# S5 input tables used inside the table loop: ten of sixteen go from on-chip memory straight into V's products

## The chip, the cores and the metric

One NeuronCore of a Trainium2 chip runs the whole program. The metric is the device time in microseconds of one execution; lower is better.

## What is computed

One layer of a hybrid encoder on 2048 tokens of width 1024, in float32: a normalisation, one input projection, two mixers side by side, an output projection, and a gated feed-forward network. Only the start of the S5 mixer matters here:

```
bur = einsum('blgc,gpc->lbgp', u, bbr)        # 32 groups g of 16 channels c, 64 states p
bui = einsum('blgc,gpc->lbgp', u, bbi)
h   = associative_scan(h[t] = a * h[t-1] + bu[t])     # complex; forward and backward
y   = Re(C h) + D u
```

The kernel cuts time into 128 blocks of 16 steps. For each pair of groups it makes a table of powers of `a` times `B`; the product of that table with the `u` values of a block is the block's input `V` to a short recursion over the 128 blocks.

## The kernel before

The program is written for a tile framework: each line names an engine, the framework places semaphores, and a list scheduler fixes the order of each engine's instructions by priority. `soon()` gives a block the priority of an early point of the program (`p0`), so that its instructions go ahead of what stands before them in the text as soon as they are ready. Each engine, and SP with the DMAs that it issues, then works through its own list in order.

A memory pool has an address range. Pools are stacked on a left and on a right side; a pool that is opened on addresses of a closed one waits for everything that used the closed one. That matters for five pools. `s0` (left) holds the weights and buffers of the projection `u_dt`. `s5cs` and `s5tab` (right) hold the constants and the working tiles of the tables. `s5v` (left) holds `V`, and `dts` and `s5vw` (left, above it) the working tiles of `dt_stage` and of `inputs`; these three take the place of `s0`. `sp` (right), which holds the working tiles of the SSD units, reaches the addresses of `dts` and `s5vw`.

The order of the work around the change:

- `norm_block` and `u_dt`, four blocks of 512 tokens: normalise, transpose on PE, project. `u` goes to DRAM (`u_d`).
- `tables(k)` for k = 0 to 15, two groups each. DVE makes `X` (three operations for each of real and imaginary part, L254 to L256). PE transposes it (L264), ACT copies the transposed table out of PSUM into `xin` (L265; one buffer), and SP stores it to DRAM (`s5xd`, 512 KB, L266). Further parts of the same call make a 64-column product for the convolution kernel `kt` (`s5cp`, L272; `s5pk`, L277 to L285) and the output table `s5O` (POOL and DVE, L238 to L243), which is stored in four pieces (L294). `kt` lives in the two buffers of `rb`, which the convolution of the SSD part needs later.
- `z_tile` for m = 0 to 3: large products that depend on none of this and fill PE's gaps.
- `dt_stage` (DVE, a chain of small operations; ACT; four small stores): the time steps of the SSD part, `tokS` and `acs_d`.
- `toeplitz`: 30 small stores of `kt` from POOL's queue (L308, L310).
- `inputs`: for eight blocks b, load `uT` from `u_d` (L318) and twice a stored table `s5xi` from `s5xd` (L322; three buffers); 16 products of 128x128x128 on PE (L329) into `s5pv`; ACT copies one half of the rows into `V` (L333), DVE the other half, reversed in time (L334).
- `recur`: 126 steps of four POOL operations on `V` (L347 to L350), paced along the SSD groups of the second half of the sequence.
- `group(1, g)`: four convolution tiles (products `pmm` into `rb`, L679, and DVE) and eight SSD units; the units load rows of `acs_d` into `rw` (L747) and begin on PE with `ptb` (L756). z tiles 4 to 7 fill in. After that come the first half of the sequence, the output projection and the feed-forward network.

Of the kernel before, what the change touches and what calls it, by code (L numbers as in the profile page):

```python
# [17 lines left out]
P = 128  # L18
# [11 lines left out]
GA = 4  # L30
ZB = ((4,), (5,), (6,), (7,))
# [71 lines left out]
class S5:  # L103
# [141 lines left out]
    def tables(self, wk, k):  # L245
# [20 lines left out]
        nc.sync.dma_start(self.xd[k], xin.rearrange("p q d m -> p (q d m)"))  # L266
# [46 lines left out]
    def inputs(self, vp, wk):  # L313
        nc = self.nc
        self.V = vp.tile([P, 2, NG5, P], F32, name="s5V")
        for b in range(8):
            uT = wk.tile([P, 8, P], F32, name="s5uT", bufs=2)
            nc.sync.dma_start(uT, self.ud[4 * b:4 * b + 4].rearrange("g h p c -> p (g h) c"))  # L318
            for kk in range(2):
                k = 2 * b + kk  # L320
                xin = wk.tile([P, 1024], F32, name="s5xi", bufs=3)
                nc.sync.dma_start(xin, self.xd[k])  # L322
                xin = xin.rearrange("p (r h g m) -> p r h g m", r=2, h=2, g=2)
                pv = self.pst("s5pv")
                for r in range(2):
                    for g in range(2):
                        o = 128 * (2 * r + g)
                        for h in range(2):
                            nc.tensor.matmul(pv[:, o:o + 128], xin[:, r, h, g],  # L329
                                             uT[:, 2 * (2 * kk + g) + h], start=(h == 0), stop=(h == 1))  # L330
                V = self.V[:, :, 2 * k:2 * k + 2, :]
                pvv = pv.rearrange("p (r g c) -> p r g c", r=2, g=2)
                nc.scalar.copy(V[0:64], pvv[0:64])  # L333
                nc.vector.tensor_copy(V[64:128, :, :, ::-1], pvv[64:128])  # L334

# [862 lines left out]
def hybrid_block_kernel(ctx: ExitStack, tc: tile.TileContext, *aps):  # L1198
# [9 lines left out]
    with ExitStack() as mix:  # L1208
# [18 lines left out]
        with pool(name="s0", bufs=1) as sp, right("s5cs") as cs:  # L1227
# [19 lines left out]
            with right("s5tab") as wk:  # L1247
                with soon():
                    for k in range(NK5):
                        s5.tables(wk, k)  # L1250
                for m in range(ZA):
                    b.z_tile(wp, ps, ht, 1, m)
        late = rs.enter_context(right("late"))
        mp = rs.enter_context(right("mp"))
        with pool(name="s5v", bufs=1) as vp, ExitStack() as xs:
            off = tc.cur_priority - p0
            with tc.high_priority(offset=off), pool(name="dts", bufs=1) as sp:
                b.dt_stage(late, sp, ps)
                with pool(name="s5vw", bufs=1) as wk:
                    s5.toeplitz(*[wk.tile([P, 1024], F32, name="s5xi", bufs=3)[0:16, 0:512].rearrange(  # L1260
                        "p (g o) -> p g o", o=16) for _ in range(2)])
                    s5.inputs(vp, wk)
            sp = rs.enter_context(right("sp"))
            xp = xs.enter_context(pool(name="s5xa", bufs=1))
            b.masks(late)
            b.sb = late.tile([P, 4, 256], F32, name="sb")
            p0 = tc.cur_priority
            for g in range(GA):
                if g == GA - 1:
                    p3 = tc.cur_priority  # L1270
                b.group(mp, wp, sp, ps, pp, ht, 1, g)
                for m in ZB[g]:
                    b.z_tile(wp, ps, ht, 1, m)
# [3 lines left out]
            with tc.high_priority(offset=tc.cur_priority - p3):  # L1277
                for j in range(2):
                    b.norm_again(xp, wp, ps, ht, j, 2 + 512 * j)
# [91 lines left out]
```

## Time and profile before

| what | value |
|---|---|
| time, median of 3 runs | 2923.3 us (2913.18 to 2929.7) |
| profiled execution: its own time | 2930.28 us |
| profiled execution: span | 2928.5 us |
| PE busy | 2701.5 us, 92% of the span |
| DVE busy | 2197.4 us, 75% |
| ACT busy | 1364.4 us, 47% |
| POOL busy | 653.9 us, 22% |
| TensorE clock granted, mean | 0.968 |

A busy PE is an upper bound: the ends of matmuls are modelled and overlap, so starts say more than durations. The spans of POOL are rough.

### The profile page before, as it was taken

Reading aid. Unit: us, or ns where it says so; the run is one execution under the profiler, and the core shown is the slowest. Engines: PE = TensorE matmul, PEld = TensorE weight load, DVE = VectorE, ACT = ScalarE, POOL = GpSimd, SP = SyncE. Lnnn points to the kernel's source line nnn. Section 1 sums busy time; section 2 is a strip of 40 time slices with the busy share of each in tenths; the row PEclk is TensorE's granted clock in tenths of the full one; section 3 lists DMA queues with packets and bytes.
Section 4 is the critical chain, followed back from the end, with each engine's and each line's share of the span. In section 5 each row is a group of like instructions: output and inputs, shape, how many; then the busy total and the mean of one; then the engine's idle time right before and its main releaser. Section 6 shows DMA issues by size and latency. Waiting matters only on the chain.

```text
span 2928.5 us, 37294 instructions
## 1 busy us (share of the span) xinstructions
PE 2701.5 (92%) x12952; PEld 2181.7 (74%) x12952; DVE 2197.4 (75%) x3255; ACT 1364.4 (47%) x2329; POOL 653.9 (22%) x1133
## 2 busy tenths in 40 slices
PE   6998899876999998899898999999999999999997
PEld 4666899765877886677776878787877777877776
DVE  5997688786786776677767777779887888656587
ACT  4542455444567665334235444446444445333254
POOL 0443499992233332111120000000000000000012
PEclk9999999988999999999998999999999999999999
DMA  4546633448455656957845234325444337456464
GB/s 129 173 133 198 168 114 121 112 128 227 134 175 162 188 163 204 252 170 201 252 141 187 79 108 137 107 77 193 149 136 130 121 131 243 160 204 194 150 233 158
DMA packets 507400, 471.55 MB, mean 161 GB/s; under 512 B 90364, under 2 KB 417356, under 8 KB 507212
## 3 DMA queue, kind: packets, MB, share of 16 engines
q1 hardware_dynamic: 504972, 463.99, 52.4%
q0 software_dynamic: 2240, 5.18, 0.7%
q8 instruction: 102, 1.67, 0.2%
q14 instruction: 86, 0.70, 0.1%
HBM read 324.37 MB, written 144.67 MB: 160 GB/s over the span
## 4 chain that ended last, share of the span: by engine, by line
PE 40%; DMA 8%; DVE 7%; issue 2%; ACT 2%; POOL 1%; SPq 0%; ACTq 0%; DVEq 0%; POOLq 0%
PE pA L1040 17%; PE pB L1040 9%; PE pD L1040 5%; PE p L444 3%; PE p L445 2%; PE p L446 2%; DMA ar<-act_d 2%; DVE ll L440 1%; DMA bs<-in_ffn_w_down_dram 1%; DMA wr<-in_ffn_w_up_dram 1%; DMA bs<-hop_d 1%; DMA wt_d<-bs 1%; PE po L846 1%; DVE tl L1027 1%; DMA tst<-in_ffn_w_down_dram 0%
## 5 line engine op out<-in xcount | busy, mean ns | idle before, releaser
L1040 PE MATMUL pA<-th,lh 128*128 128x512 f32 x1056 | 423.7, 402 | 28.3 <-ACT pc L1088 18.8
L1040 PE MATMUL pA<-tl,lh 128*128 128x512 f32 x1056 | 422.1, 400 | 4.2 <-DVE tl L1027 4.2
L1040 PE MATMUL pA<-th,ll 128*128 128x512 f32 x1056 | 420.5, 399 | 0.8 <-DVE ll L440 0.8
L444 PE MATMUL pmm<-hh,wh 128*128 128x512 f32 (+1 forms) x896 | 333.9, 373 | 3.7 <-DVE zt L706 2.4
L445 PE MATMUL pmm<-hl,wh 128*128 128x512 f32 (+1 forms) x896 | 332.7, 371 | 0.0
L446 PE MATMUL pmm<-hh,wl 128*128 128x512 f32 (+1 forms) x896 | 330.2, 369 | 0.0
L1040 PEld LDWEIGHTS pA<-th,lh 128*128 128x128 f32 x1056 | 200.6, 190 | 86.7 <-ACT pc L1088 27.4
L1040 PEld LDWEIGHTS pA<-tl,lh 128*128 128x128 f32 x1056 | 200.7, 190 | 54.2 <-DVE tl L1027 6.4
L1040 PEld LDWEIGHTS pA<-th,ll 128*128 128x128 f32 x1056 | 200.6, 190 | 50.3 <-DVE ll L440 1.6
L1040 PE MATMUL pB<-tl,lh 128*128 128x512 f32 x528 | 209.6, 397 | 1.8 <-DVE tl L1027 1.8
L1040 PE MATMUL pB<-th,lh 128*128 128x512 f32 x528 | 209.7, 397 | 1.8 <-ACT lh L439 1.6
L1040 PE MATMUL pB<-th,ll 128*128 128x512 f32 x528 | 209.2, 397 | 0.0
L1088 ACT COPY pc<-pA 128x512 f32<-128x512 f32 x204 | 116.0, 584 | 185.4 <-PE pA L1040 184.4
L444 PEld LDWEIGHTS pmm<-hh,wh 128*128 128x128 f32 x896 | 169.9, 190 | 30.2 <-issue 3.7
L445 PEld LDWEIGHTS pmm<-hl,wh 128*128 128x128 f32 x896 | 169.8, 190 | 22.6 <-issue 2.5
L764 ACT ACTIVATE Lt<-rw,tokS 128x128 f32<-128x128 f32 x512 | 157.4, 389 | 61.3 <-PE pyd L770 48.7
L446 PEld LDWEIGHTS pmm<-hh,wl 128*128 128x128 f32 x896 | 169.6, 189 | 21.3 <-issue 1.1
L692 DVE SCALAR_TENSOR_TENSOR xbc<-rb,cw,xbc 128x1024 f32<-128x1024 f32 x128 | 178.7, 1399 | 3.8 <-ACT xbc L690 2.8
L444 PE MATMUL p<-wo,yh 128*128 128x512 f32 x384 | 157.3, 410 | 22.2 <-ACT yh L439 21.3
L439 ACT CAST lh<-s 128x512 fp32r<-128x512 f32 (+3 forms) x136 | 109.1, 815 | 123.8 <-DVE s L1007 71.2
L440 DVE TENSOR_TENSOR ll<-s,lh 128x1024 fp32r<-128x1024 f32 (+3 forms) x136 | 126.3, 933 | 52.5 <-PE pA L1040 43.7
L445 PE MATMUL p<-wo,yh 128*128 128x512 f32 x384 | 155.6, 405 | 0.0
(421 smaller groups left out, 6139.0 us busy)
## 6 DMA issues: line engine op xcount, KB each, us to landing
wr<-in_ffn_w_up_dram SPq DMA_DIRECT2D x88, 512.0 KB
rw<-acs_d SPq DMA_DIRECT2D x128, 256.0 KB
wraw<-in_w_in_dram SPq DMA_DIRECT2D x52, 512.0 KB
ar<-act_d SPq DMA_DIRECT2D x32, 512.0 KB
yp_d<-cv SPq DMA_DIRECT2D x32, 512.0 KB
cv<-yp_d SPq DMA_DIRECT2D x32, 512.0 KB
tst<-hop_d SPq DMA_DIRECT2D x28, 512.0 KB
act_d<-cv SPq DMA_DIRECT2D x22, 512.5 KB
```

What stands on the lines that cost most here:

```text
L439: self.nc.scalar.copy(hi, src)
L440: self.nc.vector.tensor_tensor(lo, src, hi.bitcast(F32), ALU.subtract)
L444: mm(ps, lhs[0], rhs[0], start=first, stop=False)
L445: mm(ps, lhs[0], rhs[1], start=False, stop=False)
L446: mm(ps, lhs[1], rhs[0], start=False, stop=last)
L692: nc.vector.scalar_tensor_tensor(ac, rb[:, j:j + 1024], cw(j), ac, ALU.mult, ALU.add)
L764: nc.scalar.activation(Lt[:, d, h], rw[:, d, h], AF.Exp, bias=tk(0, d, h))
L846: nc.tensor.matmul(po[:, 2 * (g - 2 * q) + j], self.fst[:, g, 128 * j:128 * j + 128], ct[:, g], start=True, stop=True)
L1027: nc.vector.tensor_tensor(l, st[:, 0:n], h.bitcast(F32), ALU.subtract)
L1040: mm(ps, x, y, start=first and k == i == 0, stop=k == kt - 1 and i == 2, skip_group_check=not first)
L1088: self.nc.scalar.copy(t, src)
```

## The change

- `tables(k)` takes an optional `uT`. With it, the transposed table is not stored to DRAM; `input(k, xin, uT)` multiplies it with `u` at once and copies the result into `V`.
- The first KD = 6 tables go to DRAM as before, in pool `s5tab`. Then `V` is allocated, and tables 6 to 15 run in a second pool `s5tab2` on the same addresses, with `uT` loaded per pair of tables (b = 3 to 7). After tables 7, 9 and 11 the stored tables 0 to 5 are loaded again in pairs and used (`stored`; two buffers).
- The products go into a PSUM buffer of the pool `pp` (tag `tb`, two buffers) instead of `s5ps`.
- Both copies into `V` are on ACT; before, the reversed half was on DVE.
- z tiles 0 and 1 stay in the first block, 2 and 3 move into the second.
- `dt_stage` and `toeplitz` come behind all of this, and their pools `dts` and `s5tp` now take the addresses of the closed `s5vw`. `toeplitz` gets two tiles of its own. `s5cs` closes after the second block.

```diff
-        nc.sync.dma_start(self.xd[k], xin.rearrange("p q d m -> p (q d m)"))
+        if uT is None:
+            nc.sync.dma_start(self.xd[k], xin.rearrange("p q d m -> p (q d m)"))
+        else:
+            self.input(k, xin, uT)
...
+    def load_u(self, wk, b):
+        uT = wk.tile([P, 8, P], F32, name="s5uT", bufs=2)
+        self.nc.sync.dma_start(uT, self.ud[4 * b:4 * b + 4].rearrange("g h p c -> p (g h) c"))
+        return uT
+
+    def input(self, k, xin, uT):
+        nc = self.nc
+        pv = self.pp.tile([P, 512], F32, name="s5pv", tag="tb", bufs=2)
+        for r in range(2):
+            for g in range(2):
+                o = 128 * (2 * r + g)
+                for h in range(2):
+                    nc.tensor.matmul(pv[:, o:o + 128], xin[:, 4 * r + 2 * h + g].rearrange("p d m -> p (d m)"),
+                                     uT[:, 2 * (2 * (k % 2) + g) + h], start=(h == 0), stop=(h == 1))
+        V = self.V[:, :, 2 * k:2 * k + 2, :]
+        pvv = pv.rearrange("p (r g c) -> p r g c", r=2, g=2)
+        nc.scalar.copy(V[0:64], pvv[0:64])
+        nc.scalar.copy(V[64:128, :, :, ::-1], pvv[64:128])
+
+    def stored(self, wk, k):
+        xin = wk.tile([P, 8, 2, 64], F32, name="s5xi", bufs=2)
+        self.nc.sync.dma_start(xin.rearrange("p q d m -> p (q d m)"), self.xd[k])
+        return xin
...
             with right("s5tab") as wk:
                 with soon():
-                    for k in range(NK5):
+                    for k in range(KD):
                         s5.tables(wk, k)
-                for m in range(ZA):
+                for m in range(ZA // 2):
                     b.z_tile(wp, ps, ht, 1, m)
+        vp = vpo.enter_context(pool(name="s5v", bufs=1))
+        s5.V = vp.tile([P, 2, NG5, P], F32, name="s5V")
+        with right("s5tab2") as wk, pool(name="s5vw", bufs=1) as vw:
+            with soon():
+                for k in range(KD, NK5):
+                    if k % 2 == 0:
+                        uT = s5.load_u(vw, k // 2)
+                    s5.tables(wk, k, uT)
+                    j = (k - KD) // 2
+                    if k % 2 and j < KD // 2:
+                        uT = s5.load_u(vw, j)
+                        for kk in (2 * j, 2 * j + 1):
+                            s5.input(kk, s5.stored(vw, kk), uT)
+            for m in range(ZA // 2, ZA):
+                b.z_tile(wp, ps, ht, 1, m)
+        cso.close()
...
-                with pool(name="s5vw", bufs=1) as wk:
-                    s5.toeplitz(*[wk.tile([P, 1024], F32, name="s5xi", bufs=3)[0:16, 0:512].rearrange(
-                        "p (g o) -> p g o", o=16) for _ in range(2)])
-                    s5.inputs(vp, wk)
+            with pool(name="s5tp", bufs=1) as wk:
+                s5.toeplitz(*[wk.tile([P, 512], F32, name="s5z", bufs=2)[0:16].rearrange(
+                    "p (g o) -> p g o", o=16) for _ in range(2)])
```

## Rows read from the trace of the kernel before

**Rows 1.** Windows: us; busy (count) of PE, PEld, DVE, ACT, POOL; clock, DMA, GB/s.

```profile
80.00:209.00 129.00, 119.10 (x592) 77.82 (x591) 118.37 (x142) 66.86 (x163) 63.32 (x64) 0.97 0.55 159
209.00:262.00 53.00, 50.34 (x222) 36.19 (x221) 51.40 (x86) 14.97 (x38) 14.97 (x16) 0.97 0.52 151
262.00:330.00 68.00, 51.77 (x348) 48.77 (x348) 27.52 (x46) 19.26 (x32) 20.41 (x36) 0.90 0.81 237
660.00:700.00 40.00, 19.03 (x107) 14.60 (x107) 23.64 (x48) 19.82 (x50) 12.84 (x20) 0.71 0.90 251
```

**Rows 2.** Groups of instructions by line, 262 to 330 us.

```profile
L329 PE MATMUL s5pv<-s5uT,s5xi 128*128 128x128 f32 x256 | 34.7, 300 | 13.9 <-DMA s5xi<-s5xd 13.9
L334 DVE COPY s5V<-s5pv 64x512 f32<-64x512 f32 x16 | 11.0, 694 | 29.2 <-ACT s5V L333 29.1
L333 ACT COPY s5V<-s5pv 64x512 f32<-64x512 f32 x16 | 9.2, 575 | 32.8 <-PE s5pv L329 32.8
```

**Rows 3.** Timeline of PE around `inputs`: start, us, instruction, idle before it.

```profile
268.80 3.73 PE L329 MATMUL s5pv<-s5uT,s5xi 128*128 128x128 f32 x32
...
320.22 0.31 PE L444 MATMUL pmm<-hh,wh 128*128 128x342 f32 x1
...
320.68 0.32 PE L444 MATMUL pmm<-hh,wh 128*128 128x342 f32 x1
...
325.41 2.02 PE L329 MATMUL s5pv<-s5uT,s5xi 128*128 128x128 f32 x16 [0.48 <-DMA s5xi<-s5xd]
```

**Rows 4.** Groups of PE by line and shape, 268.8 to 329.3 us.

```profile
L444 PE MATMUL pmm<-hh,wh 128*128 128x342 f32 x16 | 5.4, 340 | 0.0
```

**Rows 5.** Timeline of SP's queue: stores and loads.

```profile
185.65 0.55 SPq L266 DMA_DIRECT2D s5xd<-s5xin  x1
...
210.07 1.35 SPq L565 DMA_DIRECT2D u_d<-us  x2
...
217.00 1.05 SPq L318 DMA_DIRECT2D s5uT<-u_d  x2
...
256.68 0.32 SPq L266 DMA_DIRECT2D s5xd<-s5xin  x1
...
327.46 0.80 SPq L747 DMA_DIRECT2D rw<-acs_d  x2
```

**Rows 6.** Groups of ACT by line, 80 to 262 us.

```profile
L265 ACT COPY s5xin<-s5pxt 128x512 f32<-128x512 f32 x32 | 17.2, 590 | 13.9 <-PE s5pxt L264 13.9
L272 ACT ACTIVATE s5cp<-s5ct 64x32 f32<-64x32 f32 x64 | 14.6, 228 | 5.9 <-POOL s5cp L268 5.0
L280 ACT COPY s5ks<-s5pk 64x256 f32<-64x256 f32 x16 | 5.9, 367 | 2.9 <-PE s5pk L277 1.8
L285 ACT COPY rb<-s5pk 128x64 f32<-128x64 f32 x30 | 4.9, 219 | 13.6 <-PE s5pk L283 13.5
L705 ACT ACTIVATE zt<-pmm 128x512 f32<-128x512 f32 x6 | 3.6, 596 | 18.9 <-DMA z_d<-zt 16.4 <-PE pmm L446 2.5
```

**Rows 7.** Timeline of POOL: first and last of `toeplitz`, start of `recur`.

```profile
262.83 1.49 POOL L308 DMA_DIRECT2D s5td<-rb  x2 [6.89 <-ACT rb L285]
...
284.81 0.62 POOL L310 DMA_DIRECT2D s5td<-rb  x1 [0.60 <-DMA s5td<-rb]
...
329.32 0.35 POOL L347 TENSOR_TENSOR s5r<-s5V,s5ar 128x64 f32<-128x64 f32 x1 [24.74 <-DVE s5V L334]
```

**Rows 8.** Timeline of DVE: first and last of 68 operations of `dt_stage`.

```profile
216.36 0.33 DVE L595 TENSOR_REDUCE dtm<-ident 128x1 f32<-128x64 f32 x2
...
303.16 1.23 DVE L616 TENSOR_TENSOR_SCAN dtq<-dtz,dte 128x512 f32<-128x512 f32 x1
...
314.12 0.69 DVE L633 TENSOR_TENSOR dtq<-dtq,dte 128x512 f32<-128x512 f32 x1
```

**Rows 9.** Instructions of one line: duration min/median/max in ns, first and last start.

```profile
L254 DVE TENSOR_TENSOR s5tmw<-s5pw,s5bb x32: 678/691/1759, 80.4 to 248.4; 128x512 f32<-128x512 f32 x32
```

**Rows 10.** Instructions of tile `ptb`, 300 to 450 us, same columns.

```profile
L756 PE MATMUL ptb<-ident,xbc x24: 270/272/273, 372.9 to 428.8; 128*128 128x128 f32 x24
```

More of the change, by code (lines that the diff above doesn't have):

```diff
@@ L30 @@
 GA = 4
+KD = 6
 ZB = ((4,), (5,), (6,), (7,))
@@ L243, in outer, with tables @@
             eng.tensor_tensor(out, out, tm, op)
-    def tables(self, wk, k):
+    def tables(self, wk, k, uT=None):
         nc, ident = self.nc, self.ident
@@ L311, in toeplitz @@
                               self.kt[1][112 - 16 * (l % 8):128 - 16 * (l % 8), 1 - l // 8])
-    def inputs(self, vp, wk):
-        nc = self.nc
[L315 to L334, printed above, removed]
@@ L1226, in hybrid_block_kernel @@
             "p (h g o) -> p h g o", h=2, o=16) for _ in range(2)]
-        with pool(name="s0", bufs=1) as sp, right("s5cs") as cs:
+        cso, vpo, xs = ExitStack(), ExitStack(), ExitStack()
+        cs = cso.enter_context(right("s5cs"))
+        with pool(name="s0", bufs=1) as sp:
             with right("s5prm") as sr:
@@ L1253, in hybrid_block_kernel @@
+        cso.close()
         late = rs.enter_context(right("late"))
         mp = rs.enter_context(right("mp"))
[L1255 to L1258, printed above, removed]
-                with pool(name="s5vw", bufs=1) as wk:
-                    s5.toeplitz(*[wk.tile([P, 1024], F32, name="s5xi", bufs=3)[0:16, 0:512].rearrange(
-                        "p (g o) -> p g o", o=16) for _ in range(2)])
-                    s5.inputs(vp, wk)
[L1263 to L1273, printed above, removed]
-            p1 = tc.cur_priority
-            s5.recur(vp, lambda j: tc.high_priority(offset=tc.cur_priority - p0 - int(RS * (p1 - p0) * j / P)))
-            s5.store_states()
-            with tc.high_priority(offset=tc.cur_priority - p3):
-                for j in range(2):
-                    b.norm_again(xp, wp, ps, ht, j, 2 + 512 * j)
@@ new lines, in hybrid_block_kernel @@
+        off = tc.cur_priority - p0
+        with tc.high_priority(offset=off), pool(name="dts", bufs=1) as sp:
+            b.dt_stage(late, sp, ps)
+            with pool(name="s5tp", bufs=1) as wk:
+                s5.toeplitz(*[wk.tile([P, 512], F32, name="s5z", bufs=2)[0:16].rearrange(
+                    "p (g o) -> p g o", o=16) for _ in range(2)])
+        sp = rs.enter_context(right("sp"))
+        xp = xs.enter_context(pool(name="s5xa", bufs=1))
+        b.masks(late)
+        b.sb = late.tile([P, 4, 256], F32, name="sb")
@@ new lines, in hybrid_block_kernel @@
+        p0 = tc.cur_priority
+        for g in range(GA):
+            if g == GA - 1:
+                p3 = tc.cur_priority
+            b.group(mp, wp, sp, ps, pp, ht, 1, g)
+            for m in ZB[g]:
+                b.z_tile(wp, ps, ht, 1, m)
+        p1 = tc.cur_priority
+        s5.recur(vp, lambda j: tc.high_priority(offset=tc.cur_priority - p0 - int(RS * (p1 - p0) * j / P)))
+        s5.store_states()
+        with tc.high_priority(offset=tc.cur_priority - p3):
+            for j in range(2):
+                b.norm_again(xp, wp, ps, ht, j, 2 + 512 * j)
@@ L1280, in hybrid_block_kernel @@
+        xs.close()
+        vpo.close()
         with right("s5o") as so:
```

## Prediction

> **What bounds the kernel now.** I read the busy time by window first, for the stage in which the change lies. From 80 to 262 us two engines are full: DVE is busy for 118.4 of 129 and 51.4 of 53 us, PE for 119.1 and 50.3 [rows 1]. That is the stage of `u_dt` and the tables. From 262 to 330 us nothing is full but the DMA: PE 51.8 of 68 us at a clock of 0.90, DVE 27.5, DMA share 0.81 [rows 1]. That is `inputs`. From 330 us on PE is nearly full again. So what can be won lies between 262 and 330 us.
>
> The groups of that window say what PE waits for: 13.9 us before the products of `inputs`, for the load of `s5xi` [rows 2]. DVE and ACT wait there for the products in turn (29.2 and 32.8 us). The timeline of PE gives the work itself. All 256 products lie between 268.8 and 327.4 us; 32 of them in a row take 3.73 us, 16 take 2.02 [rows 3], so 16 sets take 16 x 1.95 = 31 us. Into the same stretch the scheduler mixed 48 matmuls of the first convolution tile, 16 of each of three kinds [rows 4]; one of each kind starts every 0.46 us [rows 3], so these are 16 x 0.46 = 7.4 us. The eight transposes of `dt_stage` are about 8 x 0.12 = 1 us, an estimate from the products, which have the same shape. Of 268.8 to 329.3 us, 60.5 us, that leaves 60.5 - 31 - 7.4 - 1 = 21 us in which PE did nothing, or worked at a lower clock.
>
> DVE shows a second effect of the same loads. `dt_stage` is a chain on DVE. It begins at 216.4 us, beside the tables, but its scan starts only at 303.2, since the copies into `V`, which wait for products that wait for loads, stand ahead of it in DVE's list; it ends at 314.8 [rows 8]. The SSD units' first load of `rw` is issued at 327.46 us, just as the last product ends [rows 3, 5]: its pool takes the place of `s5vw`.
>
> **The change part by part.** *Removed:* ten stores and ten loads of 512 KB, six stores and loads stay. Ten of the 16 loads that PE waited for are gone, and the other six and all eight loads of `uT` move to a stage with a DMA share of 0.52 [rows 1]. This takes away the wait for loads. It doesn't shrink PE's work: the 31 us of products go into a stage in which PE has only 129 - 119.1 + 53 - 50.3 = 12.6 us free. They push the z tiles, PE's filler, back by as much. So the gain is the 21 us that PE lost, and up to 21 + 12.6 = 34 us if the products also fill every gap before.
>
> *Moved: when can it begin?* `V` and `uT` take the place of `s0`, so no product can run before `u_dt` has ended and its last store has landed. Before, the last store of u is issued at 210.07 us and the first load of `uT` at 217.00 [rows 5]. Table 9 was stored at 185.65 us [rows 5], so the old loop was at about table 12 then. The new loop has one buffer `xin`: table 6 fills it, tables 7 to 9 can be made up to their transposes and `X` buffers, then DVE has no more `X` to make until about 214 us (217 less the few us by which `u_dt` ends earlier when DVE and PE are free for it). What hides this is the rest of the tables: the output parts (`s5O`) need no `xin` and can be made meanwhile. PE has `u_dt` and z tiles. I cost it at nothing on PE; without that cover PE would stand from u's last store to the first `uT`, 7 us [rows 5]. The change of pool after table 5 stops DVE for a few us; PE again has `u_dt`.
>
> *Added: the chain per table on ACT.* ACT gets the reversed copy too. Per table: `xin` 2 x 0.590, two copies into `V` 2 x 0.575 (the row of the unreversed copy [rows 2]; a reversed one on DVE took 0.694), `s5cp` 4 x 0.228, `s5ks` 0.367, `rb` 2 x 0.219 [rows 6], together 1.18 + 1.15 + 0.91 + 0.37 + 0.44 = 4.05 us. From 214 us: nine tables, 36.5 us, six stored tables, 6 x 1.15 = 6.9, and eight activations of z tiles, 8 x 0.596 = 4.8 [rows 6]; 48.2 us, and with the casts of the z weights some 52. So the last table's `V` is ready at 214 + 52 = 266 us if ACT never waits. Before, the last table was stored at 256.7 us [rows 5] and `V` was complete at 329.3 [rows 7]. Bounds for the nine tables: DVE alone, six `X` of six operations of 0.691 [rows 9], 25 us, gives 240 at the earliest; the old pace, (256.7 - 185.65) / 6 = 11.8 us a table [rows 5], would give 214 + 9 x 11.8 = 320 at the latest. I take 266, nearer to the lower end, since the old pace was that of a DVE that also had `dt_stage`, norms and whole tables to do, and here the rest waits on ACT alone.
>
> *What is late next.* `rb` comes free when `toeplitz` is stored: 30 POOL issues from 262.83 to 285.43 us [rows 7], 22.6 us, and the landing, for which I take 5.6 us, the time from the end of the last store of u to the first load of `uT` [rows 5]: 266 + 28 = 294 us. Until then PE has z tiles: they end where the products begin, at 268.8 us [rows 3], and with 31 us of products ahead of them at 300. So `rb` doesn't hold the convolution, PE does; it starts at about 300, where before, with its 7.4 us of early work put in one piece, it started at 329.3 - 7.4 = 321.9. `dt_stage` now begins when `s5vw` is free, at 266 us: 68 operations whose durations add up to 37.6 us [rows 8], and 3.5 us of waits (the 13 from the scan on, 8.2 us, took 11.6), 307 us. From its end to the first load of `rw` it was 327.5 - 314.8 = 12.7 us [rows 5, 8], so `rw` loads at 320. The first SSD product on PE came at 372.9 us [rows 10], so at 352 with 21 us gained; that leaves 32 us. `recur` starts at about 295 instead of 329.3 us.
>
> Here a rule speaks against the change. Where POOL works beside it, an operation of a table on DVE takes up to 1759 ns instead of 678 [rows 9], and `recur` on POOL may now run beside the end of `dt_stage`. The Trainium skill (SBUF — State Buffer, "Who interferes with whom") says that DVE instructions with two inputs in SBUF and GpSimd instructions that read SBUF take turns, each blocked while the other runs. By that row at its worst, `dt_stage` would take 37.6 x 1759 / 678 = 98 us and end at 364, and the first SSD product would be no earlier than before; by its median of 691 ns it ends at 307 and is hidden. I take it near the lower end, since most of it is over before `recur` can begin at 295.
>
> **Sum.** 2930.3 us (the profiled execution) - 21 = 2909. The profiled execution lies 7 us over the median of the runs, so the median should be 2923.3 - 21 = 2902 us. About 0.5%, 14.6 us, is what a measurement of this kernel can tell from no change.
>
> **Rivals.**
> - *More is gained, 2880.* The products fill the 12.6 us of gaps too, and `recur` ends earlier within the SSD groups. Between 660 and 700 us, when the states are stored at a DMA share of 0.90, PE is busy for 19 of 40 us at a clock of 0.71 [rows 1]; with other work at hand half of that, 10 us, goes. 21 + 12.6 + 10 = 43 us. Against it: a schedule seldom fills all gaps, and the stores collide with something else.
> - *Late tables or a slow `dt_stage`, 2913.* If the chain takes 7.9 us a table, `V` is ready at 214 + 9 x 7.9 = 285, `rb` free at 313, and 322 - 313 = 9 us, about 10, are left; a `dt_stage` stretched by `recur` gives the same. For it: single buffers (`xin`, `s5cp`) and ACT's list in order. Time: 2913, no change that can be told.
> - *Slower, 2938: the one buffer `xin` becomes the bound.* Each table waits for the products of the one before, and these stand in PE's list behind z matmuls. The change loses when a table takes over (322 - 28 - 214) / 9 = 8.9 us; at 10.5 us, below the old 11.8, `V` comes at 308.5, `rb` at 336.5, and the convolution 15 us late. For it: the old pace. Against it: no DVE work like that is left.
>
> **How the numbers follow.** Chances: the forecast 0.45 (its own range 2890 to 2912), more gained 0.15, late tables 0.26, slower 0.14. Faster by over 0.5% (under 2908.7): 0.15 and 0.41 of the forecast's 0.45, 0.56. Same: 0.04 + 0.26 = 0.30. Slower: 0.14. The range reaches from the larger gain, 2878, to a loss of 9 us, 2932, which leaves out the upper half of the slower cases and what lies beyond the larger gain.
>
> **What would show it.** Right: between 262 and 330 us no wait of PE for `s5xi`, ten stores and loads fewer, last copies into `V` at 260 to 275 us, first convolution matmuls near 300, DVE's `dt_stage` unbroken after the last table, and everything behind shifted by some 20 us. Wrong: `V` ready after 285, PE idle between 185 and 300, a convolution that waits for `rb`, a `dt_stage` that ends after 330, or a shift that is gained at 300 and given back by 700, with the stores of the states at another place.

## The result and the profile after

The change makes the kernel slower. The kernel after takes 2956.4 us (median of four runs, 2953.6 to 2958.9), the kernel before 2925.4 in the runs beside it; 31 us by the medians, and the ratio is 1.0113, interval 1.008 to 1.0145. The spans of the profiled executions, 2951.5 and 2928.5 us, differ by 23 us. The two medians come from four runs each; in the four later sets of runs the kernel before took 2934 to 2937 us, and the kernel after was not timed there, so that the 31 us are the less certain of the two figures. Lines of the kernel after lie about five below those of before (L444 is L449, L649 is L654).

The windows of the kernel after, columns as in [rows 1], with two more of 20 us:

```profile
209.00:262.00 53.00, 52.80 (x365) 45.10 (x363) 35.11 (x43) 27.84 (x62) 13.96 (x12) 1.00 0.63 192
262.00:330.00 68.00, 26.29 (x165) 21.50 (x163) 48.65 (x90) 19.64 (x42) 34.37 (x60) 0.74 0.39 76
300.00:320.00 20.00, 0.00 (x0) 0.00 (x0) 19.45 (x39) 0.00 (x0) 8.86 (x16) 0.50 0.26 23
320.00:340.00 20.00, 8.64 (x44) 8.45 (x45) 10.03 (x17) 5.83 (x8) 16.70 (x41) 0.61 0.26 51
660.00:700.00 40.00, 19.99 (x92) 14.39 (x88) 23.25 (x39) 17.61 (x39) 0.00 (x0) 0.53 0.66 189
```

From 262 to 330 us the DMA share has fallen from 0.81 to 0.39, as it should with ten stores and ten loads gone. But PE is busy for 26.3 us where it was for 51.8 [rows 1], and from 300 to 320 us it does nothing at all, while DVE is full. The timeline of PE says what it stands for:

```profile
288.51 1.95 PE L329 MATMUL s5pv<-s5uT,s5xin 128*128 128x128 f32 x16
...
331.36 1.09 PE L654 MATMUL ptd<-ident,dtq 128*128 128x128 f32 x4 [40.90 <-DVE dtq L638]
332.24 1.06 PE L654 MATMUL ptd<-ident,dtw 128*128 128x128 f32 x4
333.12 0.65 PE L449 MATMUL pmm<-hh,wh 128*128 128x342 f32 x1
```

The last product ends at 290.5 us. The next instructions in PE's list are the eight transposes of `dt_stage`, and they wait 40.9 us for the last operation of its chain on DVE. In the kernel before the same wait is 2.3 us:

```profile
314.86 1.11 PE L649 MATMUL ptd<-ident,dtq 128*128 128x128 f32 x4 [2.32 <-DVE dtq L633]
```

The convolution stands behind the transposes in the list. It begins at 333.1 us, where the prediction had 300 and the kernel before an equivalent 321.9. The chain itself, on DVE, SP, ACT and POOL (four fences: SP's queue, DVE's first and last operation of the chain, ACT, POOL):

```profile
290.49 0.35 SPq L591 DMA_DIRECT2D dtpr<-in_ssd_dt_bias_fwd_dram  x1
...
336.87 0.81 SPq L752 DMA_DIRECT2D rw<-acs_d  x2
```

```profile
291.30 0.34 DVE L600 TENSOR_REDUCE dtm<-ident 128x1 f32<-128x64 f32 x2
...
330.40 0.81 DVE L638 TENSOR_TENSOR dtq<-dtq,dte 128x512 f32<-128x512 f32 x1
```

```profile
291.09 0.58 ACT L334 COPY s5V<-s5pv 64x512 f32<-64x512 f32 x1
325.67 0.20 ACT L644 ACTIVATE dtde<-dtend 128x4 f32<-128x4 f32 x1 [34.00 <-DVE dtend L630]
```

```profile
286.91 1.49 POOL L312 DMA_DIRECT2D s5td<-rb  x2 [8.99 <-ACT rb L289]
...
306.94 0.67 POOL L314 DMA_DIRECT2D s5td<-rb  x1
307.58 0.43 POOL L352 TENSOR_TENSOR s5r<-s5V,s5ar 128x64 f32<-128x64 f32 x1
307.98 0.78 POOL L353 TENSOR_TENSOR s5r<-s5V,s5ai 128x64 f32<-128x64 f32 x1
318.81 0.52 POOL L619 MEMSET dtz<- 128x512 f32 x1 [10.05 <-issue]
...
642.33 0.74 POOL L361 DMA_DIRECT2D s5vd<-s5V  x1 [0.29 <-POOL s5V L355]
```

The pool `dts` lies on the addresses of `s5vw`, so the first load of `dt_stage` goes out when the last product has ended; the chain takes 331.2 - 291.3 = 39.9 us and has almost nothing beside it on DVE (three operations of `toeplitz`, 0.67 us each). ACT waits 34 us of it. POOL stands 10 us of it too: `recur` begins at 307.6 us instead of 329.3 [rows 7], but a memset of `dt_stage` stands in POOL's list ahead of its third operation. `recur` stores its states 20 us earlier, from 642.3 us instead of 662.1, and no time comes of it. The first SSD product on PE comes at 389.4 us; before it was 372.9 [rows 10]:

```profile
L761 PE MATMUL ptb<-ident,xbc x24: 270/272/328, 389.4 to 446.4; 128*128 128x128 f32 x24
```

### The profile page after: what moved, and what is told of

Same layout as the page of the kernel before. It is cut to its first block, busy times and chain, and to the rows that moved or that the text cites. A ratio compares the mean times of both kernels' runs of the same rounds, so it can differ in the third digit from the quotient of the medians.

```text
span 2951.5 us, 37284 instructions
## 1 busy us (share of the span) xinstructions
PE 2692.1 (91%) x12952; PEld 2176.3 (74%) x12952; DVE 2190.5 (74%) x3239; ACT 1374.5 (47%) x2345; POOL 644.5 (22%) x1133
## 4 chain that ended last, share of the span: by engine, by line
PE 65%; DVE 13%; DMA 12%; ACT 4%; issue 3%; POOL 2%; SPq 1%; ACTq 0%; DVEq 0%; POOLq 0%
PE pA L1045 18%; PE pB L1045 9%; PE pD L1045 5%; PE pmm L449 5%; PE pmm L450 5%; PE pmm L451 5%; PE p L449 2%; PE p L450 2%; PE p L451 2%; DMA ar<-act_d 2%; DMA rw<-acs_d 1%; PE s5py L391 1%; DVE ll L445 1%; DMA s5uTo<-u_d 1%; PE pst L796 1%
## 5 line engine op out<-in xcount | busy, mean ns | idle before, releaser
L449 PE MATMUL pmm<-hh,wh 128*128 128x512 f32 (+1 forms) x896 | 333.9, 373 | 7.6 <-ACT rb L684 4.5
L449 PEld LDWEIGHTS pmm<-hh,wh 128*128 128x128 f32 x896 | 170.3, 190 | 33.5 <-ACT rb L684 5.8
L449 PE MATMUL p<-wo,yh 128*128 128x512 f32 x384 | 157.5, 410 | 21.9 <-ACT yh L444 21.9
L444 ACT CAST lh<-s 128x512 fp32r<-128x512 f32 (+3 forms) x136 | 109.1, 815 | 129.0 <-DVE s L1012 67.6
```

The lines of the kernel that those rows point to most:

```text
L444: self.nc.scalar.copy(hi, src)
L449: mm(ps, lhs[0], rhs[0], start=first, stop=False)
```

## The experiments

Theory A: what costs is `dt_stage`, whose chain now begins only behind the last product and whose transposes stand ahead of the convolution in PE's list. Rival B: the pace of the tables (8.8 us each, with one buffer `xin`) and behind it `rb`. Sixteen kernels were timed, each in runs beside the kernel before, to which the ratio is taken (its median is 2934 to 2937 us there, and 2925 us beside the kernel after). All results in one table, with what the traces show: the end of the last copy into `V`, the first SSD transpose on PE (`ptb`), and PE's busy time from 200 to 400 us.

| kernel | ratio (interval) | last V | first `ptb` | PE 200:400 |
|---|---|---|---|---|
| before | 1 | 329.2 | 372.9 | 179.9 |
| after | 1.0113 (1.008 to 1.0145) | 291.7 | 389.4 | 152.2 |
| e1 own addresses for `dts` | 1.0015 (0.9999 to 1.003) | 310.4 | 381.7 | 166.0 |
| e2 before, `dt_stage` behind | 1.0152 (1.0127 to 1.0176) | 309.2 | 415.8 | 135.5 |
| e3 `ptd` behind two tiles | 1.0010 (0.9994 to 1.0025) | 293.5 | 376.0 | 168.7 |
| e4 two `xin` | 1.0050 (1.0033 to 1.0068) | 286.1 | 386.4 | 160.9 |
| e5 six z tiles | 1.0089 (1.0054 to 1.0124) | 293.8 | 400.3 | 164.9 |
| e6 before, six z tiles | 1.0045 (1.0025 to 1.0066) | 342.4 | 385.9 | 182.6 |
| e7 e1, six z tiles | 1.0071 (1.0043 to 1.0098) | 313.0 | 391.2 | 178.0 |
| e8 e7, two `xin`, stores split | 1.0060 (1.0039 to 1.008) | 303.3 | 390.9 | 177.9 |
| e9 e8, four z tiles | 1.0023 (1.0003 to 1.0042) | 306.8 | 377.5 | 173.6 |
| e10 e3, z weights late, `dt_stage` later | 0.9992 (0.9976 to 1.0008) | 278.1 | 375.1 | 172.4 |
| e11 e3, two `xin`, stores split | 1.0021 (1.0007 to 1.0035) | 284.3 | 379.8 | 165.7 |
| e12 e10 and e11 | 0.9991 (0.997 to 1.0011) | 273.9 | 380.2 | 169.2 |
| e13 z tiles last | 1.0042 (1.0022 to 1.0061) | 276.3 | 381.6 | 165.2 |
| e14 e3 and e13 | 0.9969 (0.9949 to 0.9989) | 278.9 | 365.8 | 180.7 |
| e15 e14, two `xin`, stores split | 0.9999 (0.9979 to 1.0019) | 272.3 | 367.5 | 177.1 |
| e16 e1, e13, two `xin`, stores split | 1.0027 (1.0014 to 1.004) | 304.6 | 381.3 | 175.1 |

In fifteen of these seventeen kernels the time follows the first `ptb`: its shift against the kernel before and the difference of the two medians agree within 6 us (e2: 43 and 43 us; e14: -7 and -8.5 us). So what a kernel loses or gains is settled, for the most part, before the first SSD product. The exceptions are e12 (+7 us of shift, -4 us of time) and the kernel after (16.5 us of shift, 31 us of time); measured from the 2934 to 2937 us of the later sets, the kernel after would be 20 to 22 us slower and fit.

**The first four: which of the two it is.** e1 opens the pool `dts` between `s5v` and `s5vw`, so that it shares no address with the latter:

```diff
         s5.V = vp.tile([P, 2, NG5, P], F32, name="s5V")
+        dto = ExitStack()
+        dsp = dto.enter_context(pool(name="dts", bufs=1))
         with right("s5tab2") as wk, pool(name="s5vw", bufs=1) as vw:
...
-        with tc.high_priority(offset=off), pool(name="dts", bufs=1) as sp:
-            b.dt_stage(late, sp, ps)
+        with tc.high_priority(offset=off):
+            b.dt_stage(late, dsp, ps)
```

> The changed kernel with one thing undone: the pool of the dt stage has addresses of its own beside those of s5vw, so that its chain on DVE can run between the tables as it did before the change. Theory A (the order of the dt stage costs the time: its chain begins only when s5vw is free at 291 us, and its transposes stand in PE's list ahead of the first convolution): the 40.9 us in which PE stands before the transposes of ptd shrink to what the release of rb asks, the last copy into V at 291 to 300 us, the first convolution matmul at 312 to 321 us instead of 333, and the time falls from 2956 to 2931 to 2948. Rival B (the pace of the tables, 8.8 us each with one buffer xin, is the bound): the 38 us of the dt stage on DVE push the tables back by as much, the last copy into V at 320 us or later, and the time stays at 2950 to 2965.

e2 does the reverse to the kernel before: `dt_stage` behind `inputs`, on the addresses of their closed pool.

```diff
-            with tc.high_priority(offset=off), pool(name="dts", bufs=1) as sp:
-                b.dt_stage(late, sp, ps)
+            with tc.high_priority(offset=off):
                 with pool(name="s5vw", bufs=1) as wk:
                     s5.toeplitz(...)
                     s5.inputs(vp, wk)
+                with pool(name="dts", bufs=1) as sp:
+                    b.dt_stage(late, sp, ps)
```

> The kernel before with one part of the change alone: the dt stage is moved behind the inputs, on the addresses that their pool s5vw has left; tables, stores and loads stay as they were. Theory A: the chain on DVE begins at about 329 us, where the last product ends, PE stands for some 40 us before the transposes of ptd, the convolution starts at about 370 us instead of 329, and the time rises from 2925 to 2955 to 2970, more than the whole loss of the change. Rival B: the chain is hidden in front of the first SSD unit, and the time stays within 0.5% of 2925.

e3 leaves the chain where it is and moves only its last step, the transposes, behind the second convolution tile (the tiles `dtq` and `dtw` get a pool of their own that stays open until then):

```diff
-        for kd, src in enumerate((ln, w)):
+        self.lnw = (ln, w)
+    def dt_turn(self, ps):
+        for kd, src in enumerate(self.lnw):
             pt = ps.tile([P, 512], F32, name="ptd", tag="mm")
...
         for i, (mt, c0) in enumerate(cols):
             sl.append(self.conv_tile(mp, wp, ps, ht, half, mt, c0))
+            if mid and i == 1:
+                mid()
```

> The changed kernel with only the list of PE altered: the eight transposes of ptd, with their two copies, stand behind the first two convolution tiles, and the chain of the dt stage itself keeps its addresses and its start at 291 us. Theory A in the form that PE's list is what costs: the convolution starts when rb is free, at about 310 to 314 us instead of 333, PE stands for 20 us instead of 41, and the time falls by 15 to 21 us to 2935 to 2941. Theory A in the form that the chain itself is too late for the SSD units: the first SSD transposes stay at 389 us and the time within 0.3% of 2956. Rival B (rb or the tables hold the convolution): the first convolution matmul stays at 330 us or later, and the time at 2956.

e4 gives `xin` a second buffer:

```diff
-        xin = wk.tile([P, 8, 2, 64], F32, name="s5xin")
+        xin = (xp if xp and k % 2 else wk).tile([P, 8, 2, 64], F32, name="s5xin")
```

> The changed kernel with two buffers for the transposed table instead of one: those of the odd tables from number 7 on lie in the pool s5vw. Rival B (the one buffer sets the pace of 8.8 us a table): the pace falls to about 6.5 to 7 us, which DVE's nine operations of a table (9 x 0.69) ask, the last copy into V comes at 270 to 278 us, everything behind it 13 to 20 us earlier, and the time falls to 2936 to 2943. Theory A: the stand of PE before ptd stays at 35 to 41 us wherever it begins. If the pace has another cause (DVE's list, the stores, PE's list), the last copy stays at 288 to 294 us and the time at 2956.

e2 is the plainest. One part of the change alone, put into the kernel before, costs 1.5%, 43 us by the medians, more than the whole change. Two places came earlier than expected: with the chain no longer among the copies on DVE the last `V` came at 309.2 us instead of 329.2, so the chain began at 308 us and not at 329, and the convolution at 357.5 and not at 370. Its timeline of PE:

```profile
355.74 1.08 PE L649 MATMUL ptd<-ident,dtq 128*128 128x128 f32 x4 [47.90 <-DVE dtq L633]
356.62 1.06 PE L649 MATMUL ptd<-ident,dtw 128*128 128x128 f32 x4
357.50 0.65 PE L444 MATMUL pmm<-hh,wh 128*128 128x342 f32 x1
```

By the ratios e1 and e3 each give back about 1% of the 1.13%, from two ends: e1 moves the chain, e3 only the list. The intervals leave at least 0.5% of it; by their own medians (2938.2 and 2937.9 us beside 2956.4) it is 18 us, since the kernel before took 9 us more in their runs than beside the kernel after. In e1 the groups of PE from 200 to 420 us show the transposes without a wait, and another wait in front of the convolution:

```profile
L449 PE MATMUL pmm<-hh,wh 128*128 128x342 f32 (+1 forms) x220 | 78.7, 358 | 24.3 <-ACT rb L684 23.6 <-DVE zt L711 0.7
...
L329 PE MATMUL s5pv<-s5uT,s5xin 128*128 128x128 f32 x160 | 22.1, 296 | 9.2 <-DMA s5uT<-u_d 9.2
...
L654 PE MATMUL ptd<-ident,dtq 128*128 128x128 f32 x4 | 0.6, 272 | 0.0
```

The chain is now among the tables, and the last `V` slips from 291.7 to 310.4 us, between what A (291 to 300) and B (320 or later) had expected; the Toeplitz stores follow it to 331 us, and PE stands 23.6 us for `rb`. So theory A is right about the 41 us, and rival B has a part behind it: once `dt_stage` is out of the way, `rb` is next. e3 undoes the wait of the list and runs into the same neighbour; its groups of PE, 200 to 420 us:

```profile
L450 PE MATMUL pmm<-hh,wh 128*128 128x342 f32 (+1 forms) x227 | 81.6, 359 | 26.7 <-ACT rb L690 26.7
...
L663 PE MATMUL ptd<-ident,dtw 128*128 128x128 f32 x4 | 0.7, 287 | 2.4 <-ACT rb L690 2.4
```

Here it is ACT, which copies the convolution into `rb` and has `dt_stage`'s steps ahead of that in its own list:

```profile
329.43 0.21 ACT L645 ACTIVATE dtde<-dtend 128x4 f32<-128x4 f32 x1 [21.41 <-DVE dtend L631]
```

By its ratio e4 came out at rival B's time (from 1.0113 to 1.0050); by its own median, 2949.5 us, it is 7 us under the kernel after and missed that time. The mechanism is not rival B's either: the last `V` came 5.6 us earlier, not 13 to 20. PE's list has 48 matmuls of a z tile between the last product and the transposes there, so that the stand is 30.8 us instead of 40.9, but the first `ptb` is only 3 us earlier. Why the second buffer does so little for `V` is seen in the groups of PE in e4, 212 to 286 us:

```profile
L329 PE MATMUL s5pv<-s5uT,s5xin 128*128 128x128 f32 x155 | 20.4, 289 | 3.8 <-DMA s5uT<-u_d 3.8
L449 PE MATMUL pmm<-hh,wh 128*128 128x512 f32 x34 | 13.9, 408 | 0.0
L450 PE MATMUL pmm<-hl,wh 128*128 128x512 f32 x33 | 13.3, 403 | 0.0
```

PE waits 3.8 us in 74. It is full, and 100 of its matmuls there are z tiles (these two rows and 33 of a third kind), which nobody needs yet.

**Four with more z tiles: a wrong idea.** If PE stands, give it work. e5 to e8 take six z tiles ahead of the groups instead of four:

```diff
-ZA = 4
-ZB = ((4,), (5,), (6,), (7,))
+ZA = 6
+ZB = ((), (), (6,), (7,))
```

> The changed kernel with six z tiles of the right half ahead of the SSD groups instead of four; the two are taken from the groups, where PE is full, so the work is the same. A z tile needs neither rb nor the dt stage; two of them are 96 matmuls of 0.214 us, 20.5 us. Theory A (PE has nothing to do while the dt stage runs): they fill half of the 40.9 us in which PE stands before ptd, and the time falls by 14 to 20 us, to a ratio of 1.004 to 1.007 to the kernel before. Rival B (the tables or rb hold the convolution, and all behind it, at a fixed time): the same gain in front, but the SSD groups begin no earlier; still faster, so this run tells A's size and not A from B. If the tanh and the products of the z tiles queue behind the dt stage on ACT and DVE, PE stands again once its PSUM tiles are full, and the ratio stays at 1.009 to 1.012.

> The kernel before with six z tiles of the right half ahead of the SSD groups instead of four. The prediction counted 21 us that PE lost among the products of the inputs. If that time is there to be had by any work, the 20.5 us of two z tiles fit into it and the time falls by 10 to 20 us, to a ratio of 0.993 to 0.997, without moving a product. If the losses are short waits for loads that a list in order cannot fill, or if the z tiles only push the last products and with them the recurrence back, the ratio is 0.998 to 1.003.

> The changed kernel with addresses of its own for the dt stage, as in the first experiment, and six z tiles ahead of the SSD groups. There PE stood from 312 to 336 us for rb. Theory A: the two z tiles, 20.5 us, fill that stand, and the ratio falls from 1.0015 to 0.994 to 0.998. Rival: the z tiles are taken between the tables, push the products and the last V back by as much, and the ratio stays at 1.000 to 1.003.

> The same as the run before it, with two buffers for the transposed table, and with half of the 30 stores of the Toeplitz tiles issued on ACT, so that these take some 10 us instead of 20 on POOL. Each removes one of the delays that stood between the last table and the convolution: last V some 10 us earlier, rb some 10 us earlier behind it, the recurrence 10 to 20 us earlier. Theory A with these as what comes next: ratio 0.985 to 0.994. If the z tiles already hide all that rb holds up, the ratio is that of the run before it, and the gain of the earlier recurrence is given back between 600 and 720 us.

e8 also issues half of the Toeplitz stores on ACT (`nc.scalar.dma_start` in the second of the two lines) and has e4's buffer. Against the same kernel with four z tiles only e5 fell (from 1.0113 to 1.0089, less than expected and inside the two intervals); e6 rose by 0.45% and e7 by 0.56%, and e8 is level with e7. The work went into the stand (PE is busy for 178 us in e7, 166 in e1), but it moved the first `ptb` back (by 13 us in e6, by 9.5 us in e7), and the groups behind were not done sooner for the work taken from them. The windows 400 to 500 and 500 to 600 us, of the kernel before and then of e6:

```profile
400.00:500.00 100.00, 98.76 (x633) 90.61 (x630) 91.74 (x144) 52.91 (x125) 91.69 (x142) 1.00 0.42 129
500.00:600.00 100.00, 86.79 (x544) 79.13 (x543) 85.21 (x136) 49.37 (x113) 90.99 (x154) 0.93 0.42 116
```

```profile
400.00:500.00 100.00, 83.70 (x535) 76.53 (x534) 85.47 (x139) 48.67 (x120) 90.91 (x156) 0.91 0.35 103
500.00:600.00 100.00, 83.31 (x528) 75.78 (x527) 82.22 (x133) 48.75 (x117) 90.59 (x161) 0.91 0.45 118
```

PE is busy for 18.5 us less there (185.5 - 167.0), about the 20.5 us of the two z tiles, and the time is lost as holes. The prediction called PE nearly full from 330 us on. It is, but with the z tiles as filler: the groups go at the pace of something else. POOL is at 91% in all four windows; that it sets the pace is not shown, since no run changed its work. e9 is e8 with four z tiles again:

> The run before (own addresses for the dt stage, two buffers xin, half of the Toeplitz stores issued on ACT) with four z tiles ahead of the SSD groups again instead of six. Two z tiles more cost 0.56% in the first pair of kernels and 0.45% in the kernel before, since the groups from 400 to 600 us are not full on PE without them. If that holds here too, the ratio falls from 1.006 to 1.000 to 1.002; if the earlier V and rb are worth their 10 us each on top, to 0.993 to 0.999. If it stays at 1.004 or more, the earlier rb is lost again behind.

The ratio fell by 0.37%, to 1.0023, just above the first of its three cases; an earlier `V` and `rb` were worth nothing on top, for it is not below e1 (1.0015).

**The rest: PE's order.** e10 puts the weights of the last two z tiles on the addresses of `s5vw`, so that these cannot come before the last product. It also changes two things beside that: `toeplitz` stands ahead of `dt_stage`, with addresses of its own beside `dts`, and `dt_stage` loses its early priority. e11 adds e4's buffer and e8's split to e3; e12 is both.

```diff
-            for m in range(ZA // 2, ZA):
-                b.z_tile(wp, ps, ht, 1, m)
...
-        with tc.high_priority(offset=off), pool(name="dts", bufs=1) as sp:
-            b.dt_stage(late, sp, ps)
-            with pool(name="s5tp", bufs=1) as wk:
+        zlp = ExitStack()
+        zl = zlp.enter_context(pool(name="zl", bufs=1))
+        with pool(name="dts", bufs=1) as sp, pool(name="s5tp", bufs=1) as wk:
+            with tc.high_priority(offset=off):
                 s5.toeplitz(...)
+            b.dt_stage(late, sp, dkp, ps)
+            for m in range(ZA // 2, ZA):
+                b.z_tile(wp, ps, ht, 1, m, zl)
```

> The kernel of the third experiment (transposes of ptd behind two convolution tiles), with the weights of the last two z tiles on the addresses of s5vw, so that these tiles cannot be taken before the last product. Theory of the late tables: PE was full from 212 to 290 us, the z tiles ahead of the products pushed the last V from 266 to 291; without their 20.5 us the last V is ready at 266 to 275 us, rb at 286 to 297, the z tiles fill the stand of PE between, and the ratio falls from 1.001 to 0.992 to 0.997. Rival (the tables' own pace on DVE, POOL and the stores sets the last V): V stays at 285 us or later, the z tiles come behind it, and the ratio rises to 1.001 to 1.006.

> The kernel of the third experiment with two buffers xin and with half of the Toeplitz stores issued on ACT. There PE stood for 27 us for the release of rb behind its first 48 convolution matmuls, with ACT's list held up by the dt stage. If the stores set that stand, it shrinks by some 10 us and by 5 more from the earlier last V: ratio 0.995 to 0.999. If ACT's list sets it (the copies into rb behind the logarithm of the dt stage), the ratio stays at 1.000 to 1.003.

> All of it together: transposes of ptd behind two convolution tiles, the last two z tiles behind the last product, two buffers xin, half of the Toeplitz stores on ACT. If the 28 us that PE loses between 200 and 400 us against the kernel before are the whole loss, and PE's work there is now in an order in which it need not stand, the last V is ready at 260 to 270 us, PE's busy time from 200 to 400 us rises from 152 to 185 us or more, and the ratio falls to 0.985 to 0.995. If what the groups behind take is set by DVE and by the recurrence on POOL, the gain is given back there and the ratio is 0.997 to 1.003.

The place of the last `V` came out near that of the theory of the late tables (266 to 275 us for e10, 260 to 270 for e12): 278.1 us in e10, 273.9 in e12, against 293.5 in e3 and 284.3 in e11 with the z tiles in front. The times missed: 0.9992 and 0.9991. (e11, at 1.0021, came out where the rival had it, but the wait was again that for `dt_stage`: 19.7 us before `ptd`, which PE reached sooner.) That of e12 lies in the range of the other case, but not for its reason: PE's loss is still in front, 169.2 us of work from 200 to 400 us instead of 185. In e12 the recurrence ended 43 us before that of the kernel before (its first store at 618.6 us), and its time is level with e10's. That the earlier recurrence is worth nothing does not follow: e12's first `ptb` comes 5 us after e10's, its last at the same time (1137.3 us). Where PE stood in front is seen in e12's timelines of ACT and PE:

```profile
274.32 14.15 ACTq L315 DMA_DIRECT2D s5td<-rb  x15
288.51 1.04 ACT L445 CAST wh<-wraw 128x1024 fp32r<-128x1024 f32 x1 [14.22 <-DMA s5td<-rb]
```

```profile
289.61 0.79 PE L450 MATMUL pmm<-hh,wh 128*128 128x512 f32 x1 [16.61 <-ACT wh L445]
```

The 15 stores that were meant to free `rb` sooner occupied ACT for 14 us, and the cast of the z weights, which PE was waiting for, stood behind them. Not all of the 16.6 us is theirs: in e10, without those stores on ACT, PE stood 9.1 us at the same cast, whose weights have their addresses only behind the last product. So e13 and e14 load and cast those weights early and hold back only the matmuls, by giving them the PSUM tiles of the products of `V` in turn:

```diff
-        pt = ps.tile([P, 512], F32, name="pmm", tag="mm")
+        pt = tb.tile([P, 512], F32, name="pmz", tag="tb", bufs=2) if tb else ps.tile([P, 512], F32, name="pmm", tag="mm")
...
             for m in range(ZA // 2, ZA):
-                b.z_tile(wp, ps, ht, 1, m)
+                b.z_tile(wp, ps, ht, 1, m, pp)
```

> The changed kernel with the work of PE in another order and nothing else: the last two z tiles take the PSUM tiles of the products of V in turn with them, so that they come behind the last product on PE instead of among the tables; their weights are loaded and cast early. Theory A (PE has only the z tiles to do while the dt stage runs, and the list spends them too early): the last V moves from 291 to 270 to 276 us, the dt stage and rb with it, the z tiles fill 20 of the 41 us before ptd, and the ratio falls from 1.0113 to 1.003 to 1.007. If the late rb and not the dt stage had set the end of the stand, the gain is the same; if the tables' own pace sets the last V, it stays at 285 us or later and the ratio at 1.009 or more.

> The same with the transposes of ptd behind two convolution tiles. In the run with the z weights on the addresses of s5vw, PE stood 10 us for their cast; that wait is gone here. If it was a loss of its own, the ratio falls from 0.9992 to 0.994 to 0.997; if the dt stage on DVE and ACT holds the convolution's copies at that place anyway, it stays at 0.998 to 1.001.

> The run before it with two buffers xin, and half of the Toeplitz stores issued on SP instead of all on POOL (on ACT they held up the cast of the z weights by 14 us). Last V some 5 us earlier, rb some 10 to 15 us earlier, PE's list free of both: ratio 0.990 to 0.995. If the chain of the dt stage, 40 us on DVE behind the last V, is the bound whatever rb does, the ratio is that of the run before it within 0.2%.

> Own addresses for the dt stage, two buffers xin, z tiles behind the last product, half of the Toeplitz stores on SP. Here the chain of the dt stage is among the tables, where DVE stood idle from 200 to 220 us, and the last V is late by what it takes there. If the chain of the dt stage is what costs, and may lie at either place as long as PE has work, the last V comes at 285 to 290 us, the z tiles cover rb, and the ratio is 0.989 to 0.995. If the dt stage's stores on SP hold up the loads of the stored tables and of u again (9.2 us of PE's waiting in the first experiment), it is 0.998 to 1.002.

e13 is the changed kernel with nothing but another order on PE. Both its numbers came out as expected, `V` at 276.3 us (270 to 276) and the ratio at 1.0042 (1.003 to 1.007); its timeline shows the stand before `ptd` shrunk by 18 us:

```profile
321.81 1.11 PE L654 MATMUL ptd<-ident,dtq 128*128 128x128 f32 x4 [23.11 <-DVE dtq L638]
```

e14 has the transposes behind two convolution tiles as well, and is the one version that beats both kernels: 2927.7 us beside 2936.2, 0.9969, interval 0.9949 to 0.9989. (It is the best of sixteen, and the interval ends close to 1.) Its windows, and the longest wait of PE that is left there:

```profile
200.00:400.00 200.00, 180.74 (x1107) 160.24 (x1106) 143.27 (x211) 89.61 (x191) 119.28 (x184) 0.97 0.51 130
300.00:320.00 20.00, 15.05 (x92) 14.41 (x90) 19.37 (x29) 4.55 (x7) 7.34 (x16) 0.96 0.20 59
```

```profile
323.26 0.65 PE L450 MATMUL pmm<-hh,wh 128*128 128x342 f32 x1 [8.21 <-ACT rb L690]
```

PE works from 300 to 320 us while DVE does `dt_stage`, and the first `ptb` comes at 365.8 us, 7 us before that of the kernel before. e15 and e16 (their split stores go out on SP) missed: an earlier `rb` on top (0.9999), and the chain among the tables (1.0027), gained nothing. In e15 PE stood 12.6 us for `dt_stage` again, at 330 us: with `rb` early it reached the transposes before the chain was done. Why e15 is not level with e14 beyond that (the intervals overlap), and what holds e16 back, was not taken further.

## Why the prediction was wrong

- **What the loads cost: right.** The waits for `s5xi` are gone. In the kernel after PE waits for loads 2.4 us in all between 212 and 290 us (for `uT`), where 13.9 us had gone [rows 2]. The products begin at 211.4 us; the prediction let the loop go on at 214.
- **The last `V`: 291.7 us, not 266.** The sum on ACT, 4.05 us a table, was no bound; the tables went by at 8.8 us each (first copy into `xin` at 214.7 us, the ninth table's at 285.4: 70.7 / 8). The wrong step was that products push the z tiles back. The list did the opposite and put the z tiles between the products, and PE was full. PE's groups from 212 to 290 us of the kernel after, with 136 matmuls of z tiles (the last three rows):

```profile
L329 PE MATMUL s5pv<-s5uT,s5xin 128*128 128x128 f32 x155 | 19.1, 276 | 2.4 <-DMA s5uT<-u_d 2.4
L451 PE MATMUL pmm<-hh,wl 128*128 128x512 f32 x46 | 18.6, 404 | 0.0
L450 PE MATMUL pmm<-hl,wh 128*128 128x512 f32 x45 | 18.1, 402 | 0.0
L449 PE MATMUL pmm<-hh,wh 128*128 128x512 f32 x45 | 17.9, 398 | 0.0
```

  By the prediction's own sum this step alone takes the whole gain: `rb` free at 291.7 + 28 = 320 us, where the convolution of the kernel before stands at 321.9. e10 and e13, with two z tiles behind, had the last `V` at 278.1 and 276.3 us; the second buffer `xin` alone is worth 5.6 us (e4). The rival of the late tables had 285 us for this, the slower one 308.5.
- **`rb` and the convolution: the reason failed.** The stores took 20.7 us (22.6 predicted). But "`rb` doesn't hold the convolution, PE does" counted on z tiles until 300 us, and at 290.5 there were none left. With the transposes out of the way `rb` was the next wait, 23.6 us in e1.
- **`dt_stage`: the step that failed and made a loss of it.** Its length was right: 39.9 us where 37.6 + 3.5 were worked out. That it begins when `s5vw` is free was in the prediction too. Then it was called hidden, with 32 us to spare, since what was looked at were its readers in the SSD units. Its eight transposes, costed at 1 us of PE's time (they took 1.8, 331.4 to 333.1 us), were not placed in PE's list. They stand ahead of the convolution there, so that everything on PE behind the last product waited for the end of the chain, not for 352 us. In the kernel before they wait 2.3 us, since the chain runs beside the tables and the products. e2 put the step into the kernel before and got +1.5%; e3 took it out of the kernel after and got 1% back by the ratios, 18 us by the medians.
- **The rule on DVE and GpSimd: kept small, rightly, in part for another reason.** In `dt_stage` the last operation took 0.81 us beside `recur`, 0.69 before [rows 8], and the chain as a whole was not stretched. `recur` was held too: after its first two operations POOL stood until 318.8 us, so that it ran beside only the last 12 us of the chain. In the tables the turns show. DVE's and POOL's timelines of the kernel after:

```profile
242.61 1.54 DVE L256 TENSOR_TENSOR s5tmv<-s5pw,s5bb 128x512 f32<-128x512 f32 x1
244.26 1.58 DVE L257 TENSOR_TENSOR s5X<-s5tmw,s5tmv 128x512 f32<-128x512 f32 x1
```

```profile
242.02 1.59 POOL L239 TENSOR_TENSOR s5O<-s5pw,s5ct 128x512 f32<-128x512 f32 x1 [3.07 <-DVE s5X L257]
243.68 1.60 POOL L244 TENSOR_TENSOR s5O<-s5O,s5tmp 128x512 f32<-128x512 f32 x1
```

  That is what the Trainium skill (SBUF — State Buffer, "Who interferes with whom") states of instructions with two inputs in SBUF, and the trace agrees for operations of 128x512. Beside `recur`, whose operations are 128x64, the loss was 0.12 us on the last operation.
- **The sum.** The 21 us of the loads were not gained in time. Two steps failed, and four kernels take them apart: with both as in the change 1.0113, with the transposes moved 1.0010 (e3), with the z tiles behind the products 1.0042 (e13), with both 0.9969 (e14). The first `ptb` comes 13.4, 7.8 and 23.6 us earlier in these three than in the kernel after, so the two add up, with little over. Even e14 gains 8.5 us and not 21; what keeps the rest is open (PE still stands 8.2 us for `rb` there). From 200 to 400 us PE is busy for 27.7 us less than before, and the kernel is slower by 23 us (the spans) to 31 us (the medians). The slower rival, 2938 us by `xin`, had the right sign and the wrong mechanism; none of the rivals had PE behind `dt_stage`.
- **What comes after.** The stretch from 660 to 700 us was to give something back when `recur` ends earlier. PE is busy there for 20.0 us, before 19.0 [rows 1], although the states are stored 20 us earlier.
- **Small slips that change nothing.** In [rows 2] DVE's copies wait for those on ACT (29.1 us), not for the products. The range ends at 2878 us where the sum of the larger gain is 2880.

## What to carry to other kernels

A step that is moved has to be placed in the list of every engine that it touches, by what stands behind its instructions there: transposes of 1.8 us held PE for 41 us, since a whole stage stood behind them. When two stages share addresses, ask what the second one's chain holds up, and not only when its results are read. Work that nobody waits for (z tiles, here) belongs where an engine would stand, and it pays to check that the stage it is taken from does not need it as filler.

## What the runs showed of the hardware

- After its stand of 40.9 us PE worked at half its clock. From 300 to 320 us the granted clock is 0.50, the lower of its two levels (1.2 GHz), with no matmul at all; the first four transposes, at 331.4 us, take 1.09 us in all. In e1, where PE comes to them working, at a granted clock of 1.00, they take 0.60 (272 ns each, with overlap).
- Issuing DMAs occupies the engine that issues: 15 stores took 14.15 us of ACT's list (e12). The Trainium skill (Trainium Kernel Development and Optimization, "Key Constraints") says that issuing from several engines saves only the issue time of the sequencer; here it moved that time onto the engine that PE was waiting for.
- Issuing a store of `s5O` on SP took about 0.6 us. A row of a timeline can join instructions with a wait between them: in e1 the row of four stores at 257.0 us reads 9.21 us, but the first two end at 258.2 us and the other two begin at 265.0. The two at 234.0 us took 1.24 us in all:

```profile
233.95 1.24 SPq L298 DMA_DIRECT2D s5od<-s5O  x2
...
256.99 9.21 SPq L298 DMA_DIRECT2D s5od<-s5O  x4
```
